# Five gate products of an encoder layer by a seven-product quarter scheme, in a phase of their own

## The chip, the core and the metric

The kernel runs on one core of a Trainium2 chip. The time is device time in microseconds (us), from one launch, and lower is better. Five engines work side by side, each with its own queue: TensorE (PE, matrix products into PSUM), VectorE (DVE), ScalarE (ACT), GpSimd (POOL) and SyncE (SP, which only issues DMAs here). POOL issues DMAs too, among them ones that add to their destination.

## The reference, cut to what matters

Two layers act on 512 tokens of 1024 channels (two sequences of 256). A layer normalises its input and multiplies it by one large matrix; slices of the result feed five branches, and five further slices of 1024 columns are the gates.

```python
h = _rms_norm(x, norm_pre)
proj = h @ w_in            # 1024 x 12704; the last 5 * 1024 columns are `gates`
...                        # o_a .. o_e: two self-attentions, two convolutions, attention to a memory
outs = (o_a * silu(a_z), o_b * silu(b_z), o_c * silu(c_z), o_d * silu(d_z), o_e * silu(e_z))
g = jax.nn.sigmoid(gates.reshape(B, S, N_BRANCHES, D_MODEL))
y = g[:, :, 0] * (outs[0] @ w_branch[0])
for i in range(1, N_BRANCHES):
    y = y + g[:, :, i] * (outs[i] @ w_branch[i])
y = y @ w_out
return x + _rms_norm(y, norm_post)
```

All values are float32. The five gate products are 512 x 1024 x 1024 each; a branch projection is 512 x 512 x 1024.

## The kernel before, in words

Every product is done on TensorE in three matmuls (`mm3`, lines 125 to 128): each operand is split into a high half, a copy in the type float32r, and a low half, what that copy leaves, and high x high, high x low and low x high are summed in PSUM. A matmul here has a stationary operand of 128 x 128 and streams up to 512 columns.

*Weights.* A `Raw` (line 46) is a tile of 128 x 1024 loaded from DRAM by SP (`raw_cols`, line 265); `split` (line 304) makes its halves. ScalarE copies the high half (`copy`, line 131), VectorE subtracts to get the low half (line 301). For the gates' raws (`by_dma`, line 697) ScalarE instead writes the negative high copy (line 316) and POOL issues a DMA that adds the raw to it (line 317). There are four buffers for raws (`NRAW`) and four pairs of halves (`NSPLIT`).

*Steps.* The program is a list of `Step`s, each with its weight pieces, a function that issues its matmuls, and one that issues what follows on VectorE and ScalarE (`post`). `a_steps` (line 332) makes a tile of 128 channels x 512 tokens with the weights stationary; `b_steps` (line 344) makes tiles of 128 tokens x 512 channels with the normalised input stationary. The loop at line 1096 issues, step by step, the splits up to four raws ahead (`issue_splits`, line 1018), the matmuls, the `post`, and one portion of each background job (`bg_run`): attention items (`diff_item`, line 429; `soft_item`, line 475) and the 31-tap convolution (`taps`, line 595, a set number of taps a step). The framework then orders the instructions on each engine by its own schedule, in which an instruction whose inputs and buffer are ready may pass earlier ones that are not and puts in the semaphores. PSUM holds four accumulators (`acc`), one pair for scores, and two banks for transposes.

*Order in a layer.* Keys and values of the memory, then `e_q`, `a_q`, `a_k`, `a_v`; then for each branch its SiLU path `z` and its gates and projection (`branch`, line 679), with the inputs of the next branches between them (`ORDER`, line 741; lines 748 to 896). In `branch` the step for a channel tile m makes gate tile m (24 matmuls, `a_mm`) and projection tile m (12 matmuls), and its `post` (line 709) takes the sigmoid, multiplies and adds into `y`, which lies channel-major: channels on the partitions, 512 tokens along the row. So `y` can be used for the output projection after a split alone (`post_y`, line 729). The branch result `oh`, `ol` (line 682) is made by `post_z` right before its gates. At the end of a layer `w_out` is multiplied (line 973), then the residual and the next layer's norm follow (`finish`, line 942).

Of the kernel before, what the change touches and what calls it, by code (L numbers as in the profile page):

```python
# [16 lines left out]
D = 1024  # L17
S = 256
# [23 lines left out]
NRAW = 4  # L42
# [3 lines left out]
class Raw:  # L46


    def __init__(self, load, by_dma=False):
        self.load, self.by_dma = load, by_dma  # L50
        self.tile = self.hi = self.lo = None

# [22 lines left out]
def body(ctx, tc, xp, xs_, mp, ms, norm_pre, w_in, diff_lambda, diff_subln, sconv_w,  # L75
# [6 lines left out]
    rawp = ctx.enter_context(tc.tile_pool(name="rawp", bufs=NRAW))  # L82
# [27 lines left out]
    def f4():  # L110
        return wk.tile([128, D], F32, tag="f4", name=nm("f4"), bufs=2)

    def m2():
        return wk.tile([128, 512], F32, tag="m2", name=nm("m2"), bufs=7)
# [10 lines left out]
    def mm3(out, ah, al, bh, bl, first, last):  # L125
        nc.tensor.matmul(out, ah, bh, start=first, stop=False)  # L126
        nc.tensor.matmul(out, ah, bl, start=False, stop=False)  # L127
        nc.tensor.matmul(out, al, bh, start=False, stop=last)  # L128
# [52 lines left out]
    vecs = big.tile([128, 4, 512], F32, tag="att4", name="vecs")  # L181
# [75 lines left out]
    def raw_tile(shape):  # L257
        n = int(np.prod(shape[1:]))
        t = rawp.tile([128, 1024], F32, tag="raw", name=nm("raw"))
        v = t[:, 0:n]  # L260
        if len(shape) == 3:
            v = v.rearrange("p (k n) -> p k n", k=shape[1])
        return v
# [27 lines left out]
    def halves(src, shape, pool, tag, bufs, size):  # L291

        out = []
        n = int(np.prod(shape[1:]))
        for p in "hl":
            t = pool.tile([128, size], F32R, tag=tag + p, name=nm(tag + p), bufs=bufs)[0:shape[0], 0:n]
            if len(shape) == 3:
                t = t.rearrange("p (k n) -> p k n", k=shape[1])
            out.append(t)
        copy(out[0], src)  # L300
        ins = nc.vector.tensor_sub(out[1], src, out[0].bitcast(F32)).ins  # L301
        return out[0], out[1], ins

    def split(raw):
        if raw.tile is None:
            raise RuntimeError("weights split before their load")
        if not raw.by_dma:
            raw.hi, raw.lo, st["lo"] = halves(raw.tile, list(raw.tile.shape), wp, "w", NSPLIT, 1024)
            return
        two = []  # L310
        for p in "hl":
            t = wp.tile([128, 1024], F32R, tag="w" + p, name=nm("w" + p))
# [839 lines left out]
```

## Time and profile before

| what | value |
|---|---|
| median of 3 runs | 1671.41 us (1671.17 to 1672.8) |
| profiled execution, its own time | 1671.43 us |
| its span, first to last instruction | 1669.6 us |
| matmuls (with transposes) | 7834 |
| read from DRAM | 155.79 MB |
| mean granted clock of TensorE | 0.999 of full speed |

A profile is one execution. Its page gives busy time by engine, a chain of work followed back from the last instruction, groups of instructions by line and shape with the idle time before them and what ended it, and DMA issues. The trace behind it answers queries: waits (who waited for whom), timelines, and windows (busy time by stretch). Matmuls overlap in their pipeline, so a matmul's listed duration is longer than the time from one start to the next. An engine's idle time matters only where the work that ended last waited for it.

### The profile page before, as it was taken

How to read it: one execution, taken by the hardware profiler on the slowest of the kernel's cores; microseconds unless marked ns; L12 is line 12 of the kernel's file. 1: busy time of each engine (PE TensorE's matmuls, PEld its weight loads, DVE VectorE, ACT ScalarE, POOL GpSimd, SP SyncE). 2: the span in 40 equal slices, each digit the busy share in tenths (PEclk: the TensorE clock that was granted, in tenths of full speed). 3: DMA queues.
4: the chain of work that ended last, by engine and by line, in shares of the span. 5: the costliest groups of instructions: out<-in, count | busy, mean ns of one | idle time of the engine just before them, and what ended most of it. 6: DMA issues, size and time to landing. Idle time of an engine off the chain costs nothing.

```text
span 1669.6 us, 20710 instructions
## 1 busy us (share of the span) xinstructions
PE 1645.3 (99%) x7834; PEld 1370.2 (82%) x7834; DVE 938.1 (56%) x1616; ACT 826.6 (50%) x1440; POOL 129.6 (8%) x176
## 2 busy tenths in 40 slices
PE   7999999999999999999999999999999999999998
PEld 5888887888888878888888888888888978788886
DVE  5555535766776465432762545457676854743343
ACT  5445766423335467543553557754233354773432
POOL 3000010000101100010120001100001010000100
PEclk9999999999999999999999999999999999999999
DMA  6322453234644645665543225523356365553651
GB/s 237 105 82 70 114 126 104 77 90 119 152 126 120 150 112 127 152 147 143 177 139 101 77 64 137 140 64 90 93 122 159 106 152 123 126 139 102 157 180 66
DMA packets 154820, 203.28 MB, mean 122 GB/s; under 512 B 13983, under 2 KB 127685, under 8 KB 154720
## 3 DMA queue, kind: packets, MB, share of 16 engines
q1 hardware_dynamic: 139456, 148.92, 30.7%
q0 software_dynamic: 14656, 51.98, 14.9%
q8 instruction: 62, 1.02, 0.3%
q10 hardware_dynamic: 608, 1.06, 0.2%
q14 instruction: 38, 0.31, 0.1%
HBM read 155.79 MB, written 4.19 MB: 96 GB/s over the span
## 4 chain that ended last, share of the span: by engine, by line
PE 94%; ACT 2%; DVE 2%; issue 1%; POOL 0%; DMA 0%; POOLq 0%; DVEq 0%; ACTq 0%
PE acc L126 29%; PE acc L127 29%; PE acc L128 29%; PE tr L421 1%; ACT wh L131 1%; PE tr L236 1%; PE tr L126 1%; PE tr L128 1%; PE tr L127 1%; PE sc L438 1%; ACT att L131 1%; DVE wl L301 1%; PE sc L128 0%; PE sc L126 0%; PE sc L127 0%
## 5 line engine op out<-in xcount | busy, mean ns | idle before, releaser
L126 PE MATMUL acc<-hTh,wh 128*128 128x512 f32 x1344 | 527.1, 392 | 0.0
L131 ACT ACTIVATE wh<-raw 128x1024 fp32r<-128x1024 f32 (+2 forms) x276 | 290.6, 1053 | 475.5 <-PE acc L127 321.5
L127 PE MATMUL acc<-hTl,wh 128*128 128x512 f32 x1344 | 523.7, 390 | 0.0
L128 PE MATMUL acc<-hTh,wl 128*128 128x512 f32 x1344 | 523.3, 389 | 0.0
L301 DVE TENSOR_TENSOR wl<-raw,wh 128x1024 fp32r<-128x1024 f32 (+1 forms) x196 | 237.6, 1212 | 339.2 <-ACT wh L131 338.7
L128 PEld LDWEIGHTS acc<-hTh,wl 128*128 128x128 f32 x1344 | 252.3, 188 | 53.1
L126 PEld LDWEIGHTS acc<-hTh,wh 128*128 128x128 f32 x1344 | 252.4, 188 | 52.4
L127 PEld LDWEIGHTS acc<-hTl,wh 128*128 128x128 f32 x1344 | 252.5, 188 | 50.2
L615 DVE SCALAR_TENSOR_TENSOR att<-att,chv,att 128x488 f32<-128x488 f32 (+14 forms) x240 | 174.5, 732 | 4.0
L317 POOL DMA_DIRECT2D wl<-raw x80 | 69.3, 866 | 1109.7 <-ACT wl L316 1008.5
L128 PE MATMUL acc<-oh,wl 128*128 128x512 f32 x320 | 124.6, 389 | 0.0
L126 PE MATMUL acc<-oh,wh 128*128 128x512 f32 x320 | 124.5, 389 | 0.0
L127 PE MATMUL acc<-ol,wh 128*128 128x512 f32 x320 | 124.5, 389 | 0.0
L718 DVE TENSOR_TENSOR m<-acc,m 128x512 f32<-128x512 f32 x64 | 44.1, 689 | 99.8 <-PE acc L128 98.8
L126 PE MATMUL acc<-wh,hTh 128*128 128x512 f32 (+1 forms) x256 | 97.9, 383 | 0.0
L127 PE MATMUL acc<-wl,hTh 128*128 128x512 f32 (+1 forms) x256 | 97.3, 380 | 0.0
L128 PE MATMUL acc<-wh,hTl 128*128 128x512 f32 (+1 forms) x256 | 97.0, 379 | 0.0
L714 ACT ACTIVATE m<-acc 128x512 f32<-128x512 f32 x80 | 47.1, 589 | 86.7 <-PE acc L128 86.5
L316 ACT ACTIVATE wl<-raw 128x1024 fp32r<-128x1024 f32 x80 | 83.8, 1048 | 0.0
L127 PEld LDWEIGHTS acc<-ol,wh 128*128 128x128 f32 x320 | 60.1, 188 | 12.5
L128 PEld LDWEIGHTS acc<-oh,wl 128*128 128x128 f32 x320 | 60.1, 188 | 12.5
L126 PEld LDWEIGHTS acc<-oh,wh 128*128 128x128 f32 x320 | 60.1, 188 | 12.4
(201 smaller groups left out, 2151.1 us busy)
## 6 DMA issues: line engine op xcount, KB each, us to landing
raw<-in_w_in_dram SPq DMA_DIRECT2D x192, 512.0 KB, 3.6
wl<-raw POOLq DMA_DIRECT2D x80, 512.0 KB, 4.5
raw<-in_w_branch_dram SPq DMA_DIRECT2D x40, 512.0 KB, 3.5
raw<-in_mem_w_kv_dram SPq DMA_DIRECT2D x16, 512.0 KB, 4.6
raw<-in_w_out_dram SPq DMA_DIRECT2D x16, 512.0 KB, 4.6
raw<-in_w_in_dram SPq DMA_DIRECT2D x8, 416.0 KB, 3.7
x<-yo POOLq DMA_DIRECT2D x4, 512.0 KB, 3.1
xr<-x POOLq DMA_DIRECT2D x4, 512.0 KB, 6.6
```

The source lines that it names most:

```text
L126: nc.tensor.matmul(out, ah, bh, start=first, stop=False)
L127: nc.tensor.matmul(out, ah, bl, start=False, stop=False)
L128: nc.tensor.matmul(out, al, bh, start=False, stop=last)
L131: nc.scalar.activation(out, in_, AF.Copy)
L236: nc.tensor.transpose(tr[:, k * 128:(k + 1) * 128], src[:, (g * 4 + k) * 128:(g * 4 + k + 1) * 128], ident)
L301: ins = nc.vector.tensor_sub(out[1], src, out[0].bitcast(F32)).ins
L316: nc.scalar.activation(raw.lo, raw.tile, AF.Copy, scale=-1.0)
L317: nc.gpsimd.dma_start(raw.lo, raw.tile, accum_op=ALU.add)
L421: nc.tensor.transpose(tr[:, k * S + q * 128:k * S + q * 128 + 128], ps[q][:, k * 128:(k + 1) * 128], ident)
L615: nc.vector.scalar_tensor_tensor(av[:, :, lo:hi], uv[:, :, lo + d:hi + d], w, av[:, :, lo:hi], ALU.mult, ALU.add)
L714: nc.scalar.activation(sg, d["g"], AF.Sigmoid)
L718: nc.vector.tensor_mul(sg, d["b"], sg)
```

## The change

Each layer is now in two phases. The first makes all branch results, in the order conformer inputs (`cglu`), `a_q`, `a_k`, `e_z`, `a_v`, the latent inputs (`s_d`), half of the short convolution, the latent up-projections, its other half, then `c_z`, `a_z`, `d_z`. Each result, times its SiLU path, is stored to DRAM by POOL in four pieces of 128 x 512 (`oz`). In the first phase 36 raws a layer are now split by the accumulating DMA; gate weights no longer are, while the projection's raws (`wb`) now are.

The second phase does for each branch the gates as a product of 2 x 2 quarters: the input in quarters X11 to X22 of 256 tokens x 512 channels, the gate weights in quarters of 512 x 512. Seven products of quarters take the place of eight. `combos` makes the sums S1 to S4 of input quarters once a layer (up to sign); sums of weight quarters are made on VectorE for each branch (`plus`). The products go to three pairs of banks X, Y, Z; X goes on accumulating after ScalarE has copied it (`snap`). In the order of `seq`: X11 with W11 into X; X12 with W21 into Y; S2 with V2 into X; S1 with V1 into X; S3 with V3 into Z; S4 with W22 into X; X22 with V4 into Z. The parked result is loaded and split, the projection follows in four steps (`b_step`: c is the column half, r the row half), and `y` is now token-major, so it is transposed (`y_T`) before the output projection. Weight raws, quarters and most attention scratch share one pool of 12 tiles (`f4`) in place of separate ones, and loads are asked for a set number ahead (`ahead`). The other edits move tiles between buffers.

```diff
-    def f4():
-        return wk.tile([128, D], F32, tag="f4", name=nm("f4"), bufs=2)
-    def m2():
-        return wk.tile([128, 512], F32, tag="m2", name=nm("m2"), bufs=7)
+    def f4(dt=F32):
+        return wk.tile([128, D], dt, tag="f4", name=nm("f4"), bufs=12)
+    def m2(dt=F32):
...
     def split(raw):
-        if raw.tile is None:
+        src = raw.tile if raw.src is None else raw.src()
+        if src is None:
             raise RuntimeError("weights split before their load")
-        if not raw.by_dma:
-            raw.hi, raw.lo, st["lo"] = halves(raw.tile, list(raw.tile.shape), wp, "w", NSPLIT, 1024)
-            return
-        two = []
-        for p in "hl":
-            t = wp.tile([128, 1024], F32R, tag="w" + p, name=nm("w" + p))
-            two.append(t.rearrange("p (k n) -> p k n", k=raw.tile.shape[1]))
-        raw.hi, raw.lo = two
-        copy(raw.hi, raw.tile)
-        nc.scalar.activation(raw.lo, raw.tile, AF.Copy, scale=-1.0)
-        nc.gpsimd.dma_start(raw.lo, raw.tile, accum_op=ALU.add)
+        if raw.dest is not None:
+            raw.hi, raw.lo = raw.dest()
+        else:
+            n = int(np.prod(src.shape[1:]))
+            out = []
+            for p in "hl":
+                t = wp.tile([128, 1024], F32R, tag="w" + p, name=nm("w" + p))[:, 0:n]
+                out.append(t.rearrange("p (k n) -> p k n", k=src.shape[1]) if len(src.shape) == 3 else t)
+            raw.hi, raw.lo = out
+        if raw.by_dma:
+            copy(raw.hi, src)
+            nc.scalar.activation(raw.lo, src, AF.Copy, scale=-1.0)
+            nc.gpsimd.dma_start(raw.lo, src, accum_op=ALU.add)
+        else:
+            st["lo"] = halve(src, raw.hi, raw.lo)
+        if raw.after is not None:
+            raw.after()
...
+        def z_out(i, zoff, oname, taps=0):
+            def post(m, p):
+                t = silu(p)
                 nc.vector.tensor_mul(t, t, L[oname][:, m])
-                copy(st["oh"][:, m], t)
-                nc.vector.tensor_sub(st["ol"][:, m], t, st["oh"][:, m].bitcast(F32))
-            z = a_steps(wi, zoff, 4, hT, post_z)
-            for s_ in z:
...
+        def post_bz(m, p):
+            t = silu(p)
+            nc.vector.tensor_mul(L["cv", m], L["cv", m], t)
...
-        steps.append(Step(pkv, pe_mkv, post_mkv))
-        steps.extend(zC)
-        steps.extend(gC)
-        steps.extend(zD)
-        steps.extend(gD)
+        s_mq, s_mkv = Step(pq, pe_mq, post_mq), Step(pkv, pe_mkv, post_mkv)
+        for s_ in s_q + s_k + zE + s_v + s_d + bsteps[0] + bsteps[1]:
+            for pc in s_.pieces:
+                pc.raw.by_dma = True
+        steps.extend(cglu + s_q + s_k + zE + s_v + s_d + bsteps[0] + [s_mq, s_mkv] + bsteps[1] + zC + zA + zD)
...
+        def combos():
+            def whole(r, g):
+                t = f4().rearrange("p (k n) -> p k n", k=4)
+                h, lo = quarter(r, g)
+                nc.vector.tensor_add(t, h.bitcast(F32), lo.bitcast(F32))
+                return t
+            def keep(name, slot, x):
+                s_ = big.tile([128, 2, 4, 256], F32R, tag=f"att{slot}", name=nm("S"))
+                halve(x, s_[:, 0], s_[:, 1])
+                V[name] = (s_[:, 0], s_[:, 1])
+            a, b = whole(1, 1), whole(1, 0)
+            nc.vector.tensor_sub(a, a, b)
+            yield
+            keep("S1", 1, a)
+            c = whole(0, 0)
+            yield
+            nc.vector.scalar_tensor_tensor(a, a, -1.0, c, ALU.mult, ALU.subtract)
+            keep("S2", 2, a)
+            yield
...
+        def plus(dst, a, b, j):
+            def go():
+                if dst.v[j] is None:
+                    dst.room(j)
+                nc.vector.tensor_add(dst.v[j], a.v[j], b.v[j])
+            return go
...
+        def early(q):
+            loads = [q["11"].load(0), q["12"].load(0), q["11"].load(1), q["12"].load(1),
+                     q["22"].load(0), q["22"].load(1), q["21"].load(0), q["21"].load(1)]
+            sums = [plus(q["E"], q["11"], q["12"], 0), plus(q["E"], q["11"], q["12"], 1),
+                    plus(q["12"], q["12"], q["22"], 0), plus(q["12"], q["12"], q["22"], 1)]
+            return loads, sums
...
+            L_ = lambda *ks: [nxt[0][k] for k in ks] if nxt else []
+            A_ = lambda k: nxt[1][k] if nxt else None
+            for j in range(2):
+                add("11", qsrc("11", j), j)
+                add("21", qsrc("21", j), j, after=plus(q["11"], q["11"], q["12"], j))
+                add("V2", qsrc("11", j), j, [oz_load(j)], after=plus(q["21"], q["21"], q["11"], j))
+                add("V1", qsrc("E", j), j, [wb_load(j)])
+                add("V3", qsrc("12", j), j, [wb_load(2 + j)])
+                add("22", qsrc("22", j), j, L_(j))
+                add("V4", qsrc("21", j), j, L_(2 + j), after=A_(j))
+                add("o", lambda j=j: ozt[j], j, L_(4 + j), dest=o_room(j))
+            for j in range(4):
+                add("wb", (lambda j=j: wbt[j]), j, L_(6, 7) if j == 0 else [], after=A_(2 + j) if j < 2 else None)
+                item["wb", j].by_dma = True
+            def product(x, w, bank, first, last):
+                def pe():
+                    if first:
+                        V[bank] = [acc(), acc()]
+                    h, lo = lhs(x)
+                    for t in range(2):
+                        ts = slice(t * 128, (t + 1) * 128)
+                        for k in range(4):
+                            w_ = item[w, k // 2]
+                            mm3(V[bank][t], h[:, k, ts], lo[:, k, ts], w_.hi[:, k % 2], w_.lo[:, k % 2],
+                                first and k == 0, last and k == 3, skip_group_check=True)
+                return pe
+            def snap(name):
+                V[name] = [m2(), m2()]
+                for t in range(2):
+                    copy(V[name][t], V["X"][t])
+            def merge(name, bank, sign):
+                for t in range(2):
+                    nc.vector.tensor_add(V[name][t], V[name][t], V[bank][t])
+                for t in range(2):
+                    nc.scalar.activation(V[name][t], V[name][t], AF.Sigmoid, scale=sign)
+            def top():
+                V["g01"] = [m2(), m2()]
+                for t in range(2):
+                    nc.scalar.activation(V["g01"][t], V["X"][t], AF.Sigmoid, scale=-1.0)
+            seq = (("X11", "11", "X", True, lambda: snap("g00")),
+                   ("X12", "21", "Y", True, lambda: merge("g00", "Y", 1.0)),
+                   ("S2", "V2", "X", False, lambda: snap("g10")),
+                   ("S1", "V1", "X", False, lambda: snap("g11")),
+                   ("S3", "V3", "Z", True, lambda: merge("g11", "Z", -1.0)),
+                   ("S4", "22", "X", False, top),
+                   ("X22", "V4", "Z", False, lambda: merge("g10", "Z", 1.0)))
+            late = [item["o", 0], item["o", 1]]
+            for x, w, bank, first, post in seq:
+                pcs = [Piece(item[w, j]) for j in range(2)]
+                if w == "V4":
+                    pcs += [Piece(r) for r in late]
+                steps.append(Step(pcs, product(x, w, bank, first, x in ("X12", "S4", "X22")), post))
+            def b_step(c, r):
+                d = {}
+                def pe():
+                    d["p"] = [acc(), acc()]
+                    h, lo = V["o"]
+                    for t in range(2):
+                        ts = slice((2 * r + t) * 128, (2 * r + t + 1) * 128)
+                        for k in range(4):
+                            w_ = item["wb", 2 * c + k // 2]
+                            mm3(d["p"][t], h[:, k, ts], lo[:, k, ts], w_.hi[:, k % 2], w_.lo[:, k % 2],
+                                k == 0, k == 3)
+                def post():
+                    if n == 0 and r == 0:
+                        st["y", c] = att(4 + c)
+                    for t in range(2):
+                        y, g = st["y", c][:, 2 * r + t], V[f"g{r}{c}"][t]
+                        if n == 0:
+                            nc.vector.tensor_mul(y, d["p"][t], g)
+                            continue
+                        nc.vector.tensor_mul(g, d["p"][t], g)
+                        nc.vector.tensor_add(y, y, g)
+                    if n == NB - 1:
+                        bg.append(y_T(c, r))
+                return Step([Piece(item["wb", 2 * c + j]) for j in range(2)], pe, post)
+            steps.extend(b_step(c, r) for c in range(2) for r in range(2))
+        def y_T(c, r):
+            if c == 0 and r == 0:
+                st["yT"] = ([], [])
+            if r == 0:
+                for k, p in enumerate("hl"):
+                    st["yT"][k].append(big.tile([128, 4, 512], F32R, tag=f"hT{p}{c}", name=nm("yT" + p)))
+            yield
+            for t in range(2 * r, 2 * r + 2):
+                tr = trb()
+                for k in range(4):
+                    nc.tensor.transpose(tr[:, k * 128:(k + 1) * 128], st["y", c][:, t, k * 128:(k + 1) * 128], ident)
+                parts(tr.rearrange("p (k q) -> p k q", k=4), st["yT"][0][c], st["yT"][1][c], t)
...
+        zA[0].pre = lambda: bg.append(combos())
+        zD[1].pre = lambda: bg.append(sums_first())
+        for n in range(NB):
+            gate_branch(n)
...
-    nraw, nsp = [0], [0]
+    loads = []
+    for raw in raws:
+        loads.extend(raw.loads)
+        raw.need = len(loads)
+    nl, nsp = [0], [0]
 
     def issue_raws(most=1 << 30):
-        while nraw[0] < min(len(raws), most, nsp[0] + NRAW):
-            raws[nraw[0]].tile = raws[nraw[0]].load()
-            nraw[0] += 1
+        done = raws[nsp[0] - 1].need if nsp[0] else 0
+        ahead = raws[min(nsp[0], len(raws) - 1)].ahead
+        while nl[0] < min(len(loads), most, done + ahead):
+            loads[nl[0]]()
+            nl[0] += 1
 
...
```

## Rows read from the trace of the kernel before

**Rows 1.** Page, busy us, share of the span and instructions of each engine.

```profile
PE 1645.3 (99%) x7834; PEld 1370.2 (82%) x7834; DVE 938.1 (56%) x1616; ACT 826.6 (50%) x1440; POOL 129.6 (8%) x176
```

**Rows 2.** Page, chain of work that ended last, by engine.

```profile
PE 94%; ACT 2%; DVE 2%; issue 1%; POOL 0%; DMA 0%; POOLq 0%; DVEq 0%; ACTq 0%
```

**Rows 3.** Waits of TensorE: us in total, times, longest us.

```profile
PE tr L186 <- DMA vecs<-in_mem_norm_dram: 3.8, 1, 3.8
PE tr L236 <- DVE xm L1045: 3.8, 1, 3.8
PE acc L126 <- ACT att L131: 2.4, 3, 1.2
PE tr L421 <- ACT att L472: 2.2, 10, 0.4
```

**Rows 4.** Timeline of TensorE in a gate step: start, us, engine, line.

```profile
771.25 0.39 PE L126 MATMUL acc<-hTh,wh 128*128 128x512 f32 x1
...
773.97 0.39 PE L126 MATMUL acc<-hTh,wh 128*128 128x512 f32 x1
```

**Rows 5.** Groups of instructions by shape: TensorE; busy us, mean ns, idle before.

```profile
L126 PE MATMUL acc<-hTh,wh 128*128 128x512 f32 x1344 | 527.1, 392 | 0.0
...
L126 PE MATMUL acc<-wh,hTh 128*128 128x512 f32 x192 | 75.4, 393 | 0.0
```

**Rows 6.** Timeline of TensorE at the first layer's end: transposes.

```profile
806.61 1.03 PE L236 MATMUL tr<-ident,f 128*128 128x128 f32 x8
```

**Rows 7.** Groups by shape: ScalarE, VectorE and POOL.

```profile
L131 ACT ACTIVATE wh<-raw 128x1024 fp32r<-128x1024 f32 x266 | 281.7, 1059 | 448.5 <-PE acc L127 294.5 <-PE acc L128 98.3 <-issue 29.5
...
L301 DVE TENSOR_TENSOR wl<-raw,wh 128x1024 fp32r<-128x1024 f32 x186 | 227.5, 1223 | 330.7 <-ACT wh L131 330.3
...
L714 ACT ACTIVATE m<-acc 128x512 f32<-128x512 f32 x80 | 47.1, 589 | 86.7 <-PE acc L128 86.5
L718 DVE TENSOR_TENSOR m<-acc,m 128x512 f32<-128x512 f32 x64 | 44.1, 689 | 99.8 <-PE acc L128 98.8 <-PE tr L504 1.0
...
L396 DVE TENSOR_REDUCE mx<-sc 128x4 f32<-128x1024 f32 x32 | 38.9, 1215 | 4.8 <-PE sc L438 4.8
...
L301 DVE TENSOR_TENSOR qkl<-att,qkh 128x256 fp32r<-128x256 f32 x64 | 24.1, 417 | 8.8 <-ACT qkh L131 8.8
...
L615 DVE SCALAR_TENSOR_TENSOR att<-att,chv,att 128x494 f32<-128x494 f32 x16 | 11.7, 728 | 0.2
```

**Rows 8.** Windows: us, busy us of PE, PEld, DVE, ACT, POOL; clock, DMA, GB/s.

```profile
300.00:325.00 25.00, 24.82 (x128) 20.23 (x127) 21.43 (x39) 12.88 (x31) 1.38 (x2) 1.00 0.29 85
...
600.00:625.00 25.00, 23.50 (x109) 19.09 (x108) 17.08 (x29) 19.12 (x37) 1.74 (x2) 1.00 0.44 103
```

**Rows 9.** Page, DMA issues: KB each, median us to landing.

```profile
raw<-in_w_in_dram SPq DMA_DIRECT2D x192, 512.0 KB, 3.6
wl<-raw POOLq DMA_DIRECT2D x80, 512.0 KB, 4.5
```

**Rows 10.** Timelines of ScalarE, POOL and TensorE: one raw split by DMA.

```profile
773.99 1.06 ACT L131 ACTIVATE wh<-raw 128x1024 fp32r<-128x1024 f32 x1 [4.67 <-PE acc L127]
774.95 1.04 ACT L316 ACTIVATE wl<-raw 128x1024 fp32r<-128x1024 f32 x1
...
776.29 0.87 POOL L317 DMA_DIRECT2D wl<-raw  x1 [9.78 <-ACT wl L316]
...
777.67 0.58 ACT L714 ACTIVATE m<-acc 128x512 f32<-128x512 f32 x1
...
782.13 0.39 PE L126 MATMUL acc<-hTh,wh 128*128 128x512 f32 x1
```

**Rows 11.** Waits of all engines: us in total, times, longest us.

```profile
DVE wl L301 <- ACT wh L131: 338.7, 138, 6.9
...
DVE rc L405 <- ACT f L402: 49.6, 30, 3.3
```

## Prediction before the change was run

> **What bounds the kernel now.** I read the busy shares first: TensorE is busy 99% of the span, VectorE 56%, ScalarE 50% [rows 1]. A modelled busy share alone proves little for pipelined matmuls, so next come the chain of waits, 94% TensorE [rows 2], and TensorE's own list of waits: 7.6 us in two waits at the start, then sums of 2.4 and 2.2 us over short ones, the longest 1.2 [rows 3]. Then the timeline of one gate step: twelve matmuls of 512 columns start between 771.25 and 773.97, one per 2.72/12 = 0.2267 us [rows 4]. Their listed 0.39 us is latency; the price is the spacing. The kernel is a line of matmuls without holes, so an edit counts by the matmuls it takes away and by the holes it makes. A measurement here can tell about 0.2% (3 us) from no change.
>
> The sum is made against the profiled execution, 1671.43 us: its span of 1669.6 and 1.8 around it. It stands on the median of the runs, 1671.41.
>
> **Matmuls removed.** Per layer and branch the gates are 8 column tiles x 8 input tiles x 3 = 192 matmuls of 512 columns (640 of the 1344 on line 126 in [rows 5], and as many on each of the next two lines, over ten branches). Seven products of 256 x 512 x 512 are 7 x 2 x 4 x 3 = 168. The branch projection stays at 96, only with the operands' roles exchanged, a form that [rows 5] prices alike (393 against 392 ns). So 24 x 10 = 240 matmuls go: 240 x 0.2267 = **-54.4 us**. All of it is on the path.
>
> **Transposes added.** y is now token-major and must be transposed for the output projection: per layer 8 row and column tiles x 4 = 32 transposes, 64 in all. Eight in a row take 1.03 us with one latency of 0.27 [rows 6], so (1.03 - 0.27)/7 = 0.109 each: **+7.0 us**, on the path. Their copies to SBUF replace as many copies and subtractions of the old `post_y`, and run beside the last projections and the first output matmuls: nothing. The Trainium skill, "TensorE: Matmul & The Clock Gate", Part 4, speaks against this: it puts a transpose at about 275 ns in a kernel's context. That is the latency of the rows here, not their spacing; by it the term would be 64 x 0.275 = 17.6.
>
> **Second phase, load.** A branch is 168 + 96 = 264 matmuls, 59.8 us. VectorE: 16 subtractions and 8 sums of 1024 columns at 1.22, 6 merges and 16 multiplications or additions of 512 at 0.689: 29.4 + 15.2 = 44.5 us. ScalarE: 16 high halves at 1.06, four raws for the DMA at twice 1.06, 14 snapshots and sigmoids at 0.589: 33.7 us [rows 7]. So 74% and 56%. The densest windows of before (VectorE 21.43 of 25, ScalarE 19.12) lost TensorE 0.2 and 1.5 us [rows 8]: load alone holds nothing up.
>
> **Second phase, waits.** A product takes 5.44 us and both its weight raws; four raws are split at a time. The second raw's slot comes free when the product two before ends, and is needed 5.44 + 6 x 0.2267 = 6.8 us later; copy and subtraction take 2.3: 4.5 us spare. Bank X is snapped by ScalarE while it goes on accumulating: the first half must be copied (0.589) while the second half computes (2.72), so nothing, unless a copy of 1.06 stands ahead twice; behind the snapshot queue only copies with the 4.5 us to spare. The parked results are read back by SP 20 times (512 KB, landing in about 3.6 us [rows 9]), asked for eight loads ahead: nothing. POOL gets 40 stores and 32 more accumulating DMAs, 72 x 0.87 = 63 us [rows 10] on an engine that is 8% busy; behind a store that waits for VectorE stand only DMAs with two steps' lead.
>
> The tight place is the branch projection. Its four weight raws go through ScalarE twice and then through an accumulating DMA, and slots are free late: the first when product 6 is three quarters done, the second when it ends; between them and their use stands product 7 alone. In the trace such a raw starts its copy at 773.99, right as its slot is freed, is handed to POOL at 776.29 (2.3 us) and lands in 4.5 [rows 9, 10]: 6.8 us. Slot to use of the low half is 1.36 + 5.44 + 0.23 = 7.0 us, for either raw. The first just fits. The second finds ScalarE with 0.75 us of the first's work left and a sigmoid (0.59) ready: 0.75 + 0.59 + 6.8 = 8.1 against 7.0. That is about **1.2 us** a branch, **+12** in all. Ends: 0 (a landing under the median, the sigmoid behind) and 3 us a branch (+30), if ScalarE also does its two copies of the parked result there. I take 12, nearest to the rows' medians.
>
> **First phase.** Attention, taps and convolutions lose the gates that covered them. The densest stretch is from the last `a_v` step to the end of the first half of the short convolution: 4 + 8 steps, 17.7 + 43.5 us of matmuls (the first four are 416 columns wide), with 5.5 attention items (18 matmuls of half width at 0.113 and 8 transposes: 2.9 us each) and 2.2 of transposes: 79 us. VectorE there: 42 taps x 0.73 = 31; 5.5 items of 1.22 + 2 x 0.42 + 0.69 and half a dozen ops of 0.35 to 0.48, about 5.8, = 32; the convolution's products about 9, the latent branch's about 10, two subtractions 2.4: 84 us [rows 7]. It is 5 us over. Four accumulators let VectorE be up to two steps (10 us) late, so this costs nothing by itself. Then `zA` and `zD` add the four sums of quarters (about 15 us) and the first weight sums (5) to a VectorE that has room for about as much; what is left over goes into product 2 to 6 of the first branch. No row shows this crowding: 0 to 10 us, I take 2 a layer, **+4**, near the end where rows show no loss under 86% load [rows 8].
>
> **Sum.** 1671.4 - 54.4 + 7.0 + 12 + 4 = **1640 us**, 1.9% faster. Bounds of the unknown terms: 1624 (none) to 1664 (all); those 4.6 us of short waits of before [rows 3], and a little more of their kind, could go too: 1618.
>
> **Rivals.**
> *No holes*: all splits keep up, 1624. For it: before has as little as 5.8 us from DMA issue (776.29) to use (782.13) and no wait [rows 10]. Against it: here it is about 4.6.
> *VectorE bounds the first phase*: the 5 us over per layer, and on top its waits for exponentials, 49.6/30 = 1.65 us per item [rows 11], 5.5 x 1.65 = 9, are passed on to TensorE: 14 a layer, 1640 + 28 = 1668. For it: no window before is this dense. Against it: all raws there but two go by DMA, which takes VectorE's largest wait (338.7 us for `wh` [rows 11]) out of that stretch.
> *Slower: the projection's weights wait for the last gate.* In the order of the text those copies are issued after product 7's merge. If ScalarE keeps that order, each branch waits from the end of product 7: 0.69 + 2 x 0.58 for the merge, 2.3 + 4.5 for the raw, 8.7 us; ten of them make 1624 + 87 = 1711. It decides from 4.7 us a branch on. Against it: in the trace the copy at 773.99 ran ahead of the sigmoid at 777.67, which stands ahead of it in the text [rows 10], so the scheduler does move copies up. For it: it moves them by its own estimates, and a DMA landing is the hardest of these.
> The count of matmuls itself follows from the loops; no rival there.
>
> **Chances.** Forecast 0.48, no holes 0.24, VectorE 0.16, slower 0.12 (of the two dear cases a little lands within 0.2%). Faster 0.85, same 0.04, slower 0.11. The range 1618 to 1666 holds the first two cases with their bounds and most of the third, whose 14 us a layer may be less: about 8 in 10.
>
> **What would show it.** Right: 240 fewer `acc` matmuls at the same spacing, 64 more transposes in groups of eight; TensorE's list of waits headed by the branch projection waiting for the low half's DMA, about 1 us, up to ten times; ScalarE and VectorE at some three quarters in the second phase. Wrong: waits of 5 us and more there (order kept), or long waits of TensorE on VectorE between `a_v` and `zD` (third case), or waits on loads of parked results, which I price at nothing. A spacing other than 0.227 us would upset every term.

## The result, and the profile after

The kernel after the change takes **1652.39 us** (median; 1648.95 to 1654.4 over four runs), beside 1671.29 for the kernel before in the same session (1670.98 to 1672.8, four runs): a ratio of **0.9883, 95% interval [0.9865, 0.9901]**. It is 18.9 us faster, 1.1%. The forecast was 1640 us in a range of 1618 to 1666: the sign is right, the time lies in the range, and the gain is 60% of the 31 us forecast. The profiled execution took 1652.49 us with a span of 1650.7.

The profile's page of the kernel after: its span and busy shares, two groups of instructions (busy us and mean ns, then the idle time before and what ended it), and three DMA issues (KB each, median us to landing):

```profile
span 1650.7 us, 20815 instructions
...
PE 1608.2 (97%) x7658; PEld 1333.3 (81%) x7658; DVE 1104.1 (67%) x1788; ACT 924.0 (56%) x1562; POOL 179.9 (11%) x248
...
L130 PE MATMUL acc<-wl,att 128*128 128x512 f32 x392 | 156.8, 400 | 13.2 <-DMA wl<-f 12.2
...
L129 PE MATMUL acc<-wh,att 128*128 128x512 f32 x392 | 156.2, 399 | 1.8 <-ACT att L134 1.7
...
wl<-f POOLq DMA_DIRECT2D x104, 512.0 KB, 5.3
...
oz<-m POOLq DMA_DIRECT2D x40, 256.0 KB, 2.9
...
f<-oz SPq DMA_DIRECT2D x20, 512.0 KB, 3.5
```

Against [rows 1], TensorE has 176 matmuls fewer: 240 removed and 64 transposes added, 7834 - 240 + 64 = 7658. But its busy share went down from 99 to 97%: work went away and idle time came. One group of matmuls carries most of that idle time, and it waits for the DMA that splits a weight raw into its two halves. The median landing of these DMAs, over all 104 of 512 KB, is now 5.3 us after the issue; before it was 4.5 [rows 9]. What those that TensorE waited for took is told further below.

Waits of TensorE after (us in total, times, longest), which answer to [rows 3]:

```profile
PE acc L130 <- DMA wl<-f: 12.2, 11, 2.0
PE tr L129 <- ACT att L134: 4.5, 2, 2.2
PE tr L189 <- DMA att<-in_mem_norm_dram: 3.8, 1, 3.8
PE tr L239 <- DVE att L1260: 3.8, 1, 3.8
PE tr L203 <- DMA att<-in_diff_lambda_dram: 2.6, 1, 2.6
PE tr L431 <- ACT att L480: 2.0, 8, 0.4
...
PE tr L1088 <- DVE yTl L231: 1.3, 1, 1.3
```

The first line is new, and it is the wait that the prediction named. The second stands once in each layer: the output product of an attention item wants a transpose bank while the preparation of the latent branch's attention (`mla_prep`) has filled both. The first of the two is emptied late, because VectorE comes to its part (L224) only after a wait of 2.06 us for exponentials, and ScalarE's last copy (L134) comes after that:

```profile
271.60 0.18 DVE L415 RECIPROCAL rc<-su 128x4 f32<-128x4 f32 x1 [2.06 <-ACT f L412]
271.95 0.55 DVE L224 TENSOR_TENSOR m<-tr,cv 128x384 f32<-128x384 f32 x1
273.10 0.59 ACT L134 ACTIVATE att<-tr 32x512 f32<-32x512 f32 x1
273.74 0.39 PE L129 MATMUL tr<-f,m 128*128 128x256 f32 x1 [2.22 <-ACT att L134]
```

The next two in the list are old. The fifth and the last are new.

**Where the time went.** A list of waits gives only the time in which TensorE shows nothing in flight, and that hides some: a matmul is listed for 0.39 us while the next one may start after 0.2267. So I add up, over all pairs of neighbouring matmuls in the trace, by how much the start of the second is later than the undisturbed spacing of its kind (0.2267 us for 512 columns, 0.109 for a transpose). These "holes" are 26.8 us before and 55.7 after:

| holes of TensorE, us | before | after | growth |
|---|---|---|---|
| first 40 us | 11.2 | 15.5 | +4.3 |
| first phases (before: the rest of the kernel) | 15.5 | 20.7 | +5.2 |
| second phases, the branches | – | 17.7 | +17.7 |
| transposes of y, output projection | – | 1.8 | +1.8 |

With the matmuls that went (-54.4) and the transposes that came (+7.0), growth of 28.9 makes -18.5; measured -18.9. That this adds up is in part the way of counting, which takes the steady spacing as the price on both sides; it shows that the spacing did not change. The rows of the table hold to about 1.5 us, since they hang on the spacing taken as undisturbed. What is to be explained is 29 us of holes where the prediction had 16 (12 + 4).

**The place of the main wait.** One branch's projection, second of its four weight raws: the timelines of ScalarE, POOL and TensorE after (start us, us, engine, line; in brackets the idle time before and what ended it):

```profile
692.82 0.39 PE L129 MATMUL acc<-wh,hTh 128*128 128x512 f32 x1
```

```profile
693.35 0.58 ACT L1033 ACTIVATE m<-acc 128x512 f32<-128x512 f32 x1
693.82 1.05 ACT L134 ACTIVATE wh<-f 128x1024 fp32r<-128x1024 f32 x1
694.77 1.05 ACT L322 ACTIVATE wl<-f 128x1024 fp32r<-128x1024 f32 x1
```

```profile
696.26 0.86 POOL L323 DMA_DIRECT2D wl<-f  x1 [2.61 <-ACT wl L322]
```

```profile
699.62 0.39 PE L129 MATMUL acc<-wh,att 128*128 128x512 f32 x1
701.65 0.50 PE L130 MATMUL acc<-wl,att 128*128 128x512 f32 x1 [1.64 <-DMA wl<-f]
701.99 0.40 PE L131 MATMUL acc<-wh,att 128*128 128x512 f32 x1
702.23 0.40 PE L129 MATMUL acc<-wh,att 128*128 128x512 f32 x1
```

Read it against the prediction's chain. Product 6 makes way for product 7 at 692.82, which frees the raw's slot; the low half is due at 699.62 + 0.23 = 699.85, so there are 7.0 us, as forecast. A gate's sigmoid (L1033, 0.58 us) does stand ahead on ScalarE, as forecast, and the copy starts 1.0 us late (forecast 0.75 + 0.59 = 1.3). Copy to POOL's issue takes 693.82 to 696.26, 2.4 us (forecast 2.3). From there to the matmul 5.4 us pass (forecast 4.5). Together 8.8 against 7.0: late by 1.8. Of the three steps the landing is off by most, 0.9 us.

### The profile page after: what moved, and what is told of

Read it like the earlier page. It is cut to its first block, busy times and chain, and to the rows that moved or that the text cites. A ratio compares the mean times of both kernels' runs of the same rounds, so it can differ in the third digit from the quotient of the medians.

```text
span 1650.7 us, 20815 instructions
## 1 busy us (share of the span) xinstructions
PE 1608.2 (97%) x7658; PEld 1333.3 (81%) x7658; DVE 1104.1 (67%) x1788; ACT 924.0 (56%) x1562; POOL 179.9 (11%) x248
## 3 DMA queue, kind: packets, MB, share of 16 engines
q10 hardware_dynamic: 608, 1.06, 0.2%
## 4 chain that ended last, share of the span: by engine, by line
PE 38%; issue 7%; DMA 3%; DVE 3%; ACT 2%; POOL 0%; POOLq 0%; DVEq 0%; ACTq 0%
PE acc L130 11%; PE acc L129 11%; PE acc L131 11%; DMA wl<-f 1%; DMA f<-in_w_in_dram 1%; DVE wl L295 1%; PE tr L431 1%; ACT wh L134 1%; PE tr L239 0%; ACT att L134 0%; PE tr L1088 0%; PE tr L513 0%; PE tr L129 0%; PE tr L131 0%; PE tr L130 0%
## 5 line engine op out<-in xcount | busy, mean ns | idle before, releaser
L134 ACT ACTIVATE wh<-f 128x1024 fp32r<-128x1024 f32 (+1 forms) x276 | 288.7, 1051 | 259.1 <-PE acc L130 100.3
L295 DVE TENSOR_TENSOR wl<-f,wh 128x1024 fp32r<-128x1024 f32 (+1 forms) x164 | 199.6, 1219 | 131.6 <-ACT wh L134 128.4
L129 PE MATMUL acc<-hTh,wh 128*128 128x512 f32 x704 | 276.8, 393 | 0.0
L130 PE MATMUL acc<-hTl,wh 128*128 128x512 f32 x704 | 275.6, 391 | 0.0
L131 PE MATMUL acc<-hTh,wl 128*128 128x512 f32 x704 | 275.0, 391 | 0.0
L130 PE MATMUL acc<-wl,att 128*128 128x512 f32 x392 | 156.8, 400 | 13.2 <-DMA wl<-f 12.2
L626 DVE SCALAR_TENSOR_TENSOR att<-att,chv,att 128x496 f32<-128x496 f32 (+13 forms) x240 | 164.6, 736 | 0.7
L129 PE MATMUL acc<-wh,att 128*128 128x512 f32 x392 | 156.2, 399 | 1.8 <-ACT att L134 1.7
L131 PE MATMUL acc<-wh,att 128*128 128x512 f32 x392 | 154.6, 395 | 0.0
L134 ACT ACTIVATE wh<-att 128x1024 fp32r<-128x1024 f32 x60 | 63.2, 1056 | 111.6 <-PE acc L131 104.0
L129 PE MATMUL acc<-wh,S 128*128 128x512 f32 x320 | 124.5, 389 | 0.0
L130 PE MATMUL acc<-wl,S 128*128 128x512 f32 x320 | 124.5, 389 | 0.0
L131 PE MATMUL acc<-wh,S 128*128 128x512 f32 x320 | 124.5, 389 | 0.0
L129 PEld LDWEIGHTS acc<-wh,hTh 128*128 128x128 f32 x496 | 93.1, 188 | 17.7 <-DVE m L701 0.8
```

The costliest lines, as they stand in the source:

```text
L129: nc.tensor.matmul(out, ah, bh, start=first, stop=False, **kw)
L130: nc.tensor.matmul(out, ah, bl, start=False, stop=False, **kw)
L131: nc.tensor.matmul(out, al, bh, start=False, stop=last, **kw)
L134: nc.scalar.activation(out, in_, AF.Copy)
L295: return nc.vector.tensor_sub(lo, src, hi.bitcast(F32)).ins
L626: nc.vector.scalar_tensor_tensor(av[:, :, lo:hi], uv[:, :, lo + d:hi + d], w, av[:, :, lo:hi], ALU.mult, ALU.add)
```

## The experiments

Every experiment is an edit of the kernel after, timed in three or five rounds against the kernel before on the same chip, in three sessions (before: 1671.38, 1671.48, 1671.52). The first kernel is the one after, unchanged. It ran in the first session, beside the three that take the splits or the small constants alone; the other experiments are compared with it across sessions, for which the three times of the kernel before speak.

### The kernel after again

> The changed kernel again, beside the others of this group. All theories: 1649 to 1655 us, TensorE waiting about 12 us in some eleven waits for the accumulating DMAs of the projection's weights, and about 3 us once at the start.

1650.50 us (1649.87 to 1651.92), 0.9876 [0.9863, 0.989]. Below, "the control" is this kernel. Its span was 1649.0 and its holes 54.1 us.

### The projection's splits on VectorE, all of them and the second half

```diff
             for j in range(4):
                 add("wb", (lambda j=j: wbt[j]), j, L_(6, 7) if j == 0 else [], after=A_(2 + j) if j < 2 else None)
-                item["wb", j].by_dma = True
```

> The four raws of each branch projection are split by VectorE's subtraction, not by the accumulating DMA; nothing else. Theory A (the projection's weights arrive late because of the DMA's landing): the eleven waits, 12.2 us, go, and with them the slow matmuls right after the longest of them; some 17 us of holes in all, so 1635 us (1632 to 1640). Theory B (VectorE is the next bound: four more subtractions of 1.22 make 49.4 us of a branch's 59.8): waits of TensorE for that subtraction take their place, over 8 us in sum, and the time stays at 1643 or more.

1633.62 us (1631.42 to 1634.19), 0.9774 [0.976, 0.9787]: **16.9 us under the control.** The waits for `wl` by DMA are gone from TensorE's list, and its holes fell from 54.1 to 34.6. A window of one branch (us; busy us of PE, PEld, DVE, ACT, POOL; granted clock, DMA share, GB/s), first of the kernel after, then of this one:

```profile
577.00:638.70 61.70, 60.16 (x266) 49.49 (x264) 41.99 (x46) 32.19 (x39) 3.46 (x4) 1.00 0.57 154
```

```profile
565.00:625.00 60.00, 60.00 (x266) 49.67 (x266) 46.69 (x50) 28.84 (x35) 0.00 (x0) 1.00 0.40 123
```

The same 266 matmuls take 61.70 us in the one and 60.00 in the other, with no idle time left. VectorE carries the subtractions at 78% load without holding anything up: the DMA had spared an engine that had room. The edit takes away the DMA, its issue and ScalarE's second copy together; how much each weighs is told by the chain above, not by this run.

The second kernel leaves the DMA only the last two of the four raws:

```diff
-                item["wb", j].by_dma = True
+                item["wb", j].by_dma = j >= 2
```

> Only the first two of the four raws of each branch projection are split by VectorE; the last two keep the DMA. Theory A, in the form that only the first two have a single product between their slot and their use: the same gain as with all four, within 2 us of it, about 1635 us. If the DMA's own length counts wherever it is used: half of the 12.2 us of waits stays, about 1643 us.

1633.85 us (1633.01 to 1635.99), 0.9777 [0.9764, 0.9791], the same as the one before. The last two raws cost nothing by DMA; the loss is made by the first two alone, whose slots come free with a single product to go.

### Small constants asked for earlier

In the first 40 us, TensorE's third wait (2.6 us, for a transpose of `diff_lambda`) is new. The theory was that the loads of small constants share the memory with weight loads that now start earlier. The edit asks for four of them at an earlier point, where none were asked for:

```diff
-            some_consts(0)
+            some_consts(4)
```

> At the start, POOL issues four small constant loads (short convolution, convolution bias, norm gain and bias) one stage earlier, ahead of the six weight loads' bulk; nothing else. Theory S (they land late, 5 us after issue, because the larger pool lets six more weight loads start at 18 us): TensorE's wait of 2.6 us at 29 us goes, and the slow matmuls after it, about 4.4 us in all: 4 us less than the control. Rival L (the wait is for diff_lambda, as the profile names it, which is not moved): the wait stays and the time is the control's within 1 us.

1649.97 us (1648.69 to 1651.26), 0.9872 [0.9858, 0.9885]: 0.5 us under the control, which the intervals can't tell from nothing. The wait for `diff_lambda` is gone, but another one of 1.8 us stands in its place, for a product of VectorE (third line):

```profile
PE tr L239 <- DVE att L1260: 4.0, 1, 4.0
PE tr L189 <- DMA att<-in_mem_norm_dram: 3.7, 1, 3.7
...
PE tr L194 <- DVE m L224: 1.8, 1, 1.8
```

A miss. The wait of 2.6 us is also not the same in every execution: it is 2.3 us in the control, and the kernel with all the projection's splits on VectorE, whose edit changes nothing at the start, shows this in its place:

```profile
PE tr L203 <- DMA att<-in_conf_ln_b_dram: 0.5, 1, 0.5
```

With both edits together:

```diff
-                item["wb", j].by_dma = True
...
-            some_consts(0)
+            some_consts(4)
```

> The projection's raws by VectorE and the constants earlier, together. If both theories hold and the holes are apart from each other, the gains add up: 1652 - 17 - 4 = 1631 us. If the holes move elsewhere: 1640 or more.

1632.61 us (1631.92 to 1633.78), 0.9768 [0.9754, 0.9783]: as with the splits on VectorE alone. What makes the start longer, by 4 us in the kernel after and by less in some of the others, stays open.

### Transposes twice

Every transpose of y is done twice into the same place, which prices it by itself:

```diff
-                for k in range(4):
+                for k in (0, 1, 2, 3, 0, 1, 2, 3):
                     nc.tensor.transpose(tr[:, k * 128:(k + 1) * 128], st["y", c][:, t, k * 128:(k + 1) * 128], ident)
```

> Each transpose of y before the output projection is done twice (the second overwrites the first with the same values): 64 more transposes, nothing else. Row price of 0.109 us each: 7 us more than the changed kernel, about 1659. By the Trainium skill (TensorE: Matmul & The Clock Gate, Part 4, about 275 ns): 17.6 us more, about 1670.

1655.89 us (1654.23 to 1656.41), 0.9905 [0.989, 0.992]. That is 5.4 us over the control; by spans it is 3.4, with 3.6 us fewer holes (50.5 against 54.1). Together these make the 7.0 of 64 x 0.109, as they must by the way of counting; the finding in it is that the doubled transposes left no holes of their own. TensorE's timeline prices them directly, kernel after first, then this one:

```profile
772.24 1.03 PE L1088 MATMUL tr<-ident,att 128*128 128x128 f32 x8
```

```profile
771.60 1.91 PE L1088 MATMUL tr<-ident,att 128*128 128x128 f32 x16
```

Eight more take 1.91 - 1.03 = 0.88 us, 0.11 each. At 0.27 us each, for which a single transpose is listed, the edit would have added 17 us.

### Eight products in the new frame

What would the change be worth without its removed product? Here the two phases, the token-major layout, the parked results and the transposes stay, and the gates are eight plain products of quarters (no sums of quarters, each gate's sigmoid straight from its bank). Shown is the list of products; the list of weights shrinks with it, and the two jobs that make the sums go:

```diff
-            seq = (("X11", "11", "X", True, lambda: snap("g00")),
...
-                   ("X22", "V4", "Z", False, lambda: merge("g10", "Z", 1.0)))
+            seq = (("X11", "11", "X", True, None), ("X12", "21", "X", False, lambda: gate("g00", "X")),
+                   ("X21", "11", "Y", True, None), ("X22", "21", "Y", False, lambda: gate("g10", "Y")),
+                   ("X11", "12", "Z", True, None), ("X12", "22", "Z", False, lambda: gate("g01", "Z")),
+                   ("X21", "12", "W", True, None), ("X22", "22", "W", False, lambda: gate("g11", "W")))
```

> The same two phases, parked results, token-major gates and transposes, but the gates as eight plain products of quarters: no sums of quarters, 8 raws split for a branch's gates where the seven need 14. Theory M (the seven products give their matmuls' worth): 240 matmuls more, 54.4 us, so 1652 + 54 = 1706 (1700 to 1710). Rival W (part of the gain was eaten by the seven products' own sums and splits, 44.5 us of VectorE in 59.8 a branch): the eight lose fewer holes, so only 35 to 48 us more, 1687 to 1700.

1703.23 us (1702.69 to 1706.51), 1.0194 [1.0179, 1.0209]: **52.7 us over the control**, and 31.8 over the kernel before. By spans it is 51.9 us, with 2.6 us fewer holes (51.5), where 240 matmuls at the steady spacing make 54.4: the removed product gives what its matmuls cost, within 3 us. And the frame alone costs 31.8 us; counted by parts, 7.0 for transposes and 51.5 - 26.8 = 24.7 for holes. In the kernel after it is 7.0 + 28.9 = 35.9. So 32 to 36 of some 54 us, three fifths to two thirds of the gain, go back into the frame.

### First-phase splits on VectorE

```diff
-        for s_ in s_q + s_k + zE + s_v + s_d + bsteps[0] + bsteps[1]:
-            for pc in s_.pieces:
-                pc.raw.by_dma = True
```

> In the first phase all raws are split by VectorE, as most were in the kernel before, in place of 36 a layer by the accumulating DMA. Theory V (VectorE is the tight engine of the first phase): 36 x 1.22 = 44 us more of VectorE in some 370 us a layer, already 84 us in 79 in the densest stretch; TensorE waits for VectorE there, 10 us or more a layer: 1672 or more. Rival S (ScalarE is the tight one there, since each DMA raw costs it a second copy of 1.04 us): 37 us less ScalarE a layer, and the holes at the attention items, about 8 us a layer, shrink: 1640 to 1650.

1657.12 us (1656.4 to 1657.85), 0.9916 [0.9899, 0.9932]: 6.6 us over the control. Two windows of a first phase in which ScalarE is busy too, kernel after first, then this one (columns as above):

```profile
300.00:325.00 25.00, 24.61 (x131) 20.06 (x131) 17.67 (x38) 17.13 (x41) 2.77 (x4) 1.00 0.49 126
325.00:350.00 25.00, 23.94 (x126) 18.32 (x127) 22.42 (x54) 23.18 (x60) 6.47 (x9) 1.00 0.59 147
```

```profile
300.00:325.00 25.00, 25.00 (x126) 20.01 (x125) 24.20 (x50) 18.18 (x45) 1.91 (x4) 1.00 0.36 106
325.00:350.00 25.00, 21.59 (x110) 16.05 (x109) 23.84 (x47) 16.39 (x40) 3.38 (x4) 0.86 0.20 64
```

With the splits by DMA, VectorE has 22.4 of 25 us there and ScalarE 23.2, and TensorE loses 1.06. With them on VectorE it has 24.2 and 23.8, and TensorE loses 3.4 in the second window and runs at a lower granted clock for part of it. New waits for VectorE stand in its list (5.5 us for its subtractions, line 295). So VectorE is a bound in the first phase if it also splits those weights, and as the change is, it is not. Its load by itself does not decide this: earlier in the first phase of the kernel after, in the 31-tap convolution, it is busy all the time and TensorE loses nothing:

```profile
125.00:150.00 25.00, 25.00 (x137) 21.52 (x136) 25.00 (x50) 19.00 (x38) 3.55 (x4) 1.00 0.64 163
```

### More turns for attention preparation

The 2.2 us waits for ScalarE come where `mla_prep` fills two transpose banks in one go. The edit lets it yield after each, on top of the splits on VectorE:

```diff
-                if t % 2 == 1:
-                    yield
+                yield
```

> The projection's raws by VectorE (as in the first experiment) and, besides, the latent branch's preparation gives way after every token tile, not after every second one, so that its two transposes in a row no longer hold both transpose banks while ScalarE is in an attention item's exponentials. Theory T (TensorE's longest wait of the first phase, 2.2 us a layer at the attention item's output product, is for a transpose bank that ScalarE has yet to empty): that wait and the slow matmuls after it go, 2 x (2.2 + 1.5) us: 1626 us (1624 to 1629). Rival N (ScalarE is simply full there, so the wait only moves to the next transpose): 1631 to 1635, with as much waiting for ScalarE as before.

**1627.62 us (1626.22 to 1628.2), 0.9732 [0.9719, 0.9746]**: 6.0 us under the kernel with the splits on VectorE alone, and 2.7% under the kernel before. It is the fastest of all. The head of TensorE's list, where both waits of 2.2 us are gone and the start alone is left:

```profile
PE tr L239 <- DVE att L1258: 3.8, 1, 3.8
PE tr L189 <- DMA att<-in_mem_norm_dram: 3.7, 1, 3.7
PE tr L203 <- DMA att<-in_diff_lambda_dram: 2.4, 1, 2.4
PE acc L129 <- ACT att L134: 1.8, 4, 0.8
```

Its holes are 31.4 us: 15.3 at the start, 16.0 in the first phases, none in the second. The waits listed were 4.4 us, yet 6.0 came back, across sessions. The two profiled executions are only 3.3 us apart (spans 1629.7 and 1626.4). They differ in chance, too: this one has the long wait at the start, which the other lacks, and the other shows no fall of the clock behind its waits of 2.2 us, where the control does (last section). So the 6.0 is not split into wait, clock and chance here.

One more edit on top leaves the `d_c` projection's splits to VectorE too:

```diff
-        for s_ in s_q + s_k + zE + s_v + s_d + bsteps[0] + bsteps[1]:
+        for s_ in s_q + s_k + zE + s_v + bsteps[0] + bsteps[1]:
```

> As e8, and the four latent-input raws of a layer are split by VectorE, not by the DMA, which takes 4 x 1.04 us from ScalarE and puts 4 x 1.22 on VectorE in the same stretch. If ScalarE is the tighter of the two there: 1 to 4 us less than e8. If VectorE is: 2 to 6 us more.

1634.16 us (1633.67 to 1636.22), 0.9776 [0.9763, 0.9789]: 6.5 us slower again. New lines, for VectorE's subtraction and for ScalarE's copies, head what follows the start:

```profile
PE sc L446 <- DVE f L295: 2.4, 2, 1.2
PE tr L431 <- ACT m L134: 1.9, 2, 1.0
```

The granted clock falls too: it is 0.93 between 275 and 300 us, where the kernel without this last edit has 1.00. VectorE's four subtractions a layer come at a loss in this stretch of the first phase; in the second phase forty cost nothing. One of the two new lines is for ScalarE, so that VectorE alone makes the loss is not shown.

## Why the prediction was right, and where it was off

**Matmuls removed, -54.4: right.** The count is exact, the spacing is still 0.2267, and the eighth product by itself measured 51.9 by spans and 52.7 by times.

**Transposes, +7.0: right.** Eight more take 0.88 us, 0.11 each, and doubling them all cost 5.4 us by times. The spacing, not the latency, is the price, where they stand in a stream.

**The branch projection, +12: right place and mechanism, too small; it measured 17.7 in the trace and 16.9 by taking it away.** By the forecast's own terms a branch is late by 8.1 - 7.0 = 1.1, so 11 in all; it wrote 1.2 and 12. Ten of the eleven waits are for the second raw, as forecast. Their matmuls start 12.5 us late in all (0.73 to 2.18 each): close to the 11, with the landing longer than assumed and ScalarE earlier. The ten landings are 4.4 to 6.3 us, 4.9 in the median, where the term took 4.5. The page's 5.3 is not theirs: it mixes in the first phase and the third and fourth raws, which land in 7.2 and 8.3 us in the median and cost nothing. Three pieces were not in the term. The first raw, which "just fits", was late once, by 1.5 us, when it took 7.1 us to land. Each matmul that waited is followed by one at 0.34 instead of 0.23 us, 1.2 us in all. The rest, about 2.5, is mostly the granted clock behind the longest wait, told of below. The 12.2 of the list of waits agrees with the forecast only by chance, since it leaves such parts out.

**The first phase, +4: right size by luck, wrong reason.** 5.2 was measured. The prediction looked for it in a VectorE at its limit after `a_v` and in sums left over for the first branch. It put 84 us of VectorE's work into 79 there. The trace has 47.3 in such a stretch, from the first step of 416 columns on (columns as above):

```profile
242.40:321.40 79.00, 75.73 (x409) 64.12 (x408) 47.30 (x129) 56.82 (x138) 13.49 (x17) 1.00 0.57 127
```

Of the 31 us of taps that it counted there, 4.4 are left; the others ran before, from 115 us on, where VectorE is full and TensorE loses nothing (the window from 125 to 150 us above). So the load that the term was made from is not there. The larger part of the 5.2 is the two waits of 2.2 us for a transpose bank, which the sum did not have. What is behind them is nearer to the second rival than to the forecast: VectorE's wait for exponentials, 2.06 us here, is passed on to TensorE, once a layer and not once an attention item. When the two waits were removed, the first phases' holes went back to 16.0, against 15.5 before.

**Not in the sum: the start, +4.3, and the transposes of y, +1.8.** I costed the new pool of twelve tiles at nothing ahead of the first phase. It lets six weight loads start at 18 us (before, the first loads of `w_in` started at 36.78), and among the first transposes are waits that were not there. SP's queue in the kernel after (start us, us):

```profile
18.26 21.41 SPq L271 DMA_DIRECT2D f<-in_w_in_dram  x6
```

That these loads cause the wait was not shown, and the wait differs between executions. The transposes of y wait once, 1.3 us, for VectorE's subtraction: I had called their copies hidden without asking what hides the first of them.

So the sum of the forecast, -54.4 + 7.0 + 12 + 4, needs 5.7 for the projection, 1.2 for the first phase, 4.3 and 1.8: 13.0 together, and the difference between forecast and measurement is 12.4.

**The rivals.** *No holes* (1624) did not happen, but the kernel with two edits comes to 1627.6, so the frame allows it. *VectorE bounds the first phase* (1668) is not what happens: TensorE has no long waits on VectorE there. It is near, though: each of the two edits that gave VectorE more there cost some 6.5 us, and the two waits of 2.2 us come by the way that this rival names. *The projection's weights wait for the last gate* (1711) is false: copies ran ahead as they had before, and no wait is over 2.0 us in the list. Waits on loads of parked results, which would have upset the price of nothing, don't stand in the list at all.

## What to carry to other kernels

Cost the removed work and the new frame apart: here the work was worth some 54 us, and the frame that made it possible took 36 of them; two small edits brought 23 of these back (1650.50 to 1627.62). Where a transfer has no slack, take not its median landing of the old kernel but its spread beside the transfers that will run with it (4.4 to 7.1 us for the raws that were waited for, where the median of before was 4.5), or give the work to an engine that has idle time in that stage, and look at what waits for that engine there: VectorE took the splits for nothing in the second phase and not in the first. Read lost time from the starts of the matmuls, since the list of waits showed 12.2 us of the projection's 17.7.

## What the runs showed of the hardware

**A wait can cost more than it lasts.** Windows around two waits of over 2 us in the kernel after (columns as above; the granted clock is the third number from the end, a share of 2.4 GHz):

```profile
29.00:32.00 3.00, 0.38 (x4) 0.14 (x3) 2.08 (x6) 0.42 (x1) 2.00 (x4) 1.00 0.80 233
32.00:36.00 4.00, 4.00 (x15) 3.23 (x16) 2.88 (x7) 2.52 (x4) 0.67 (x2) 0.65 0.02 7
```

```profile
1327.30:1330.00 2.70, 0.68 (x4) 0.31 (x3) 0.00 (x0) 1.73 (x3) 0.68 (x1) 1.00 0.97 230
1330.00:1334.00 4.00, 4.00 (x12) 3.14 (x11) 0.69 (x1) 0.00 (x0) 0.18 (x1) 0.57 1.07 256
```

In the 3.0 and 2.7 us of the first lines TensorE was busy 0.38 and 0.68. In the 4 us behind them the mean granted clock is 0.65 and 0.57, a mix of full speed and the lower level of 1.2 GHz; behind the wait at 1329.65 the matmuls from 1330.59 to 1333.57 start 0.42 to 0.43 us apart where 0.227 is usual. Behind the wait of 1.64 us at 701.65, shown above, they were back at 0.23 to 0.24 after one start. Nor does every wait of over 2 us bring the clock down. Behind the wait that ends at 273.74 it stayed at full speed in the kernel after (first line), and in the control, behind the same wait, it fell (second line); behind the projection's wait at 1330 it was the other way round, 0.57 in the kernel after and 1.00 in the control:

```profile
273.80:277.80 4.00, 4.00 (x21) 3.39 (x21) 2.18 (x6) 2.99 (x5) 0.00 (x0) 1.00 0.09 26
```

```profile
271.80:275.80 4.00, 4.00 (x14) 3.35 (x15) 2.18 (x6) 2.70 (x5) 0.00 (x0) 0.59 0.10 29
```

TensorE started 21 matmuls in the one stretch and 14 in the other. This fits the wider spread of the kernel after (5.4 us between its runs, 1.8 for the kernel before in the same session, and a mean clock of 0.995 to 0.999), but which run had which wait was not followed up.

**The landing of an accumulating DMA depends on what surrounds it.** 512 KB from SBUF to SBUF took 4.5 us in the median before [rows 9]. In the kernel after, the four of a branch are issued some 2 to 3.5 us apart each time. Beside the loads for the next branch they took 4.9 to 8.5 us (those from 692 to 702 us: first line, and the loads: second line); in the last branch of the second layer, with no such loads, all four took 4.4 to 4.8 (from 1569 to 1579, third line):

```profile
wl<-f POOLq DMA_DIRECT2D x4, 512.0 KB, 6.9
f<-in_w_branch_dram SPq DMA_DIRECT2D x2, 512.0 KB, 7.7
```

```profile
wl<-f POOLq DMA_DIRECT2D x4, 512.0 KB, 4.5
```

So their own spacing is not what lengthens them; that the loads do is the likely reading, and no run changed the loads alone.

**Reading a bank in the midst of its accumulation cost nothing that can be seen.** ScalarE copies bank X three times a branch between products that go on adding to it, and no wait of the second phase is left in the list when the projection's splits are off the DMA.
